# The second half of each modulation dot product on GpSimd and ScalarE instead of VectorE

## The chip, the cores and the metric

The program runs on one core of one Trainium2 chip. Its engines are TensorE (PE; PEld is its weight load), VectorE (DVE), ScalarE (ACT), GpSimd (POOL) and SyncE (SP), which issues most of the transfers. The metric is the device time of one execution in microseconds (us), the median of a few executions.

## What is computed

One transformer layer on 512 tokens of width 2048 in fp32: a modulation vector from the conditioning row `c`, a mixer (attention heads and a linear recurrence), and a layer of 16384 experts of which each token uses 128. Only the first lines matter here:

```python
sc = jax.nn.silu(c)                      # (1, 2048)
mod = sc @ w_ada[l] + b_ada[l]           # w_ada: (2048, 6 * 2048)
sh1, sc1, ga1, sh2, sc2, ga2 = jnp.split(mod, 6, axis=-1)
h = _rmsnorm(x, g_mix[l]) * (1.0 + sc1[:, None, :]) + sh1[:, None, :]
mix = _hybrid_mixer(h, w_in[l], ...)     # proj = h @ w_in, attention, recurrence, w_out
x = x + ga1[:, None, :] * mix
h = _rmsnorm(x, g_ffn[l]) * (1.0 + sc2[:, None, :]) + sh2[:, None, :]
x = x + ga2[:, None, :] * _peer(h, ...)
```

## The kernel before

**The dot products.** `w_ada` lies transposed, so that one block of 128 rows holds 128 outputs of `mod`, one in each partition, with their 2048 weights in a row. `ada(s, k)` makes the 128 outputs of block k of part s, and there are 96 such calls. Each call, a *pair* below, loads two tiles `araw` of 128x1024 (512 KB), one for each half of the 2048 weights, and reduces each against `sil`, which holds silu(c) in every partition: one VectorE instruction (L145, SCALAR_TENSOR_TENSOR) multiplies and sums along the row into `acc`. L147 adds the two sums and the bias into `mod`, and for two of the parts L151 makes a scale `gs` of it.

**Two stages use it.** In the prologue 32 pairs run, those of sh1 and sc1, in a loop over 16 blocks k of the model width. There `araw` has NAR = 5 buffers. Each k also normalizes and scales one block of `x` (L209 on ScalarE), splits it into a high and a low part (`hh` by a ScalarE cast at L210, `hlo` by a VectorE subtraction at L211), streams one tile of `w_pro`, which is split in the same way (`shi` at L91, `slo` at L92), and does 24 matmuls (L214, L217). In the mixer stage the other 64 pairs run, a few at a time by `some_ada` between the projections. There `araw` has two buffers. Each projection (`proj`, L299) streams two tiles of `w_in` through 4 buffers `raw` and 3 buffers for `shi` and `slo`, with 24 matmuls of 128x512 a tile. The values of these 64 pairs are wanted only later, at the output projection and beyond.

**The order.** The tile framework's scheduler sets the order on each engine from its own model of the program. The loads of `araw` (L144) and of the streams (L96) all stand in SyncE's queue, which issues in order: an instruction there that waits for a buffer holds back all that stand behind it. ScalarE, VectorE and GpSimd also work in order. GpSimd does nothing in the first 850 us but set constants; later it copies `dh` and `dl` (L674, L675) and issues the gathers of the expert layer.

Of the kernel before, what the change touches and what calls it, by code (L numbers as in the profile page):

```python
# [14 lines left out]
AF = mybir.ActivationFunctionType  # L15
OP = mybir.AluOpType
# [40 lines left out]
def program(ctx: ExitStack, tc: tile.TileContext, a):  # L57
    nc = tc.nc
    V, A, PE, G = nc.vector, nc.scalar, nc.tensor, nc.gpsimd
# [12 lines left out]
    def col(n, i):  # L72
        return cols[:, COFF[n] + i:COFF[n] + i + 1]
# [31 lines left out]
    def rstd(pool, ss, n, scale):  # L105
        v = pool.tile([128, 16], F32, name="rs", tag="rs", bufs=4)[:, :n]
        A.activation(v, ss, AF.Sqrt, bias=eps, scale=scale)
        V.reciprocal(v, v)
        return v
# [4 lines left out]
    acc = const.tile([128, 6, 16, 2], F32, name="acc")  # L114
# [16 lines left out]
    sil = silp.tile([128, D], F32, name="sil")  # L131
    crow = []
    for half in range(2):
        r = raw.tile([128, 1024], F32, name="raw")[:1]
# [5 lines left out]
    def ada(s, k):  # L140
        for half in range(2):
            r = araw[0].tile([128, 1024], F32, name="araw", bufs=NAR if araw[0] is pro_pool[0] else None)
            n0 = (s * 16 + k) * 128
            nc.sync.dma_start(r, a["w_ada"][n0:n0 + 128, half * 1024:half * 1024 + 1024])  # L144
            V.scalar_tensor_tensor(out=r, in0=r, scalar=1.0, in1=sil[:, half * 1024:half * 1024 + 1024],  # L145
                                   op0=OP.mult, op1=OP.mult, accum_out=acc[:, s, k, half:half + 1])
        V.scalar_tensor_tensor(out=mod[:, s, k:k + 1], in0=acc[:, s, k, 0:1], scalar=acc[:, s, k, 1:2],  # L147
                               in1=b_ada[:, s, k:k + 1], op0=OP.add, op1=OP.add)
        if s in (1, 4):
            g = col("g_mix" if s == 1 else "g_ffn", k)  # L150
            V.scalar_tensor_tensor(out=gsc[s - 1][:, k:k + 1], in0=mod[:, s, k:k + 1], scalar=1.0, in1=g,  # L151
                                   op0=OP.add, op1=OP.mult)
# [3 lines left out]
    def some_ada(n):  # L156
        for _ in range(n):
            if late_ada:
                ada(*late_ada.pop(0))
# [18 lines left out]
    with tc.tile_pool(name="pro", bufs=1, reuse_waits="tile") as pro:  # L178
# [7 lines left out]
        for t in range(NT):  # L186
# [7 lines left out]
            r = rstd(pro, ss, 1, 1.0 / D)  # L194
# [11 lines left out]
        for k in range(KC):  # L206
            ada(1, k)
            ada(0, k)
            A.activation(xT[:, k], xT[:, k], AF.Identity, bias=mod[:, 0, k:k + 1], scale=gsc[0][:, k:k + 1])  # L209
            A.copy(hh[k], xT[:, k])  # L210
            V.tensor_tensor(out=hlo[k], in0=xT[:, k], in1=hh[k], op=OP.subtract)  # L211
            wh, wl = stream(a["w_pro"][k], PRO * 128)
            for i, (l, r) in enumerate(three(wfh, wfl, hh[k], hlo[k])):
                PE.matmul(pf[:8], l[:, k * 8:k * 8 + 8], r, start=(k == 0 and i == 0), stop=(k == KC - 1 and i == 2))  # L214
            for j in range(PRO):
                for i, (l, r) in enumerate(three(wh, wl, hh[k], hlo[k])):
                    PE.matmul(pacc[j], l[:, j * 128:j * 128 + 128], r, start=(k == 0 and i == 0),  # L217
                              stop=(k == KC - 1 and i == 2))
# [43 lines left out]
    for t in range(NT):  # L262
# [3 lines left out]
                           scalar=-1.0, in1=bf_row[:, None, :].to_broadcast([128, NT, 8]), op0=OP.mult, op1=OP.subtract)  # L266
# [290 lines left out]
    with tc.tile_pool(name="wk2", bufs=12, reuse_waits="tile") as wk2:  # L557
        for q in range(4):
            pr = bank()
            for k4 in range(4):  # L560
                k = q * 4 + k4
# [79 lines left out]
    for h in range(H):  # L641
# [6 lines left out]
        for half in range(2):  # L648
            p = pbank()
            for hv in range(2):  # L650
                wh, wl = stream(a["w_q"][h * 2 + half, hv])
                for k8 in range(8):
                    k = hv * 8 + k8
# [12 lines left out]
            s = tp.tile([128, S], F32, name=f"sc{half}", bufs=2)  # L666
# [72 lines left out]
    with tc.tile_pool(name="tp0", bufs=1, reuse_waits="tile") as tp0:  # L739
# [9 lines left out]
        for h in range(H):  # L749
# [7 lines left out]
                               in1=se[:, 1].rearrange("p h k -> p (h k)"), op0=OP.mult, op1=OP.add)  # L757
# [112 lines left out]
    with tc.tile_pool(name="dz", bufs=1, reuse_waits="tile") as dz:  # L870
        Fs = []
        sets = {}
        for hf, (t, h0) in enumerate(((1, 0), (1, 64), (2, 0), (2, 64), (0, 0), (0, 64))):
            ws = dz.tile([128, NB, TH], F32, name="ws")
            for t4 in range(TH // 4):
# [5 lines left out]
                                in1=oT[t][:, 0, t0:t0 + 4, None].to_broadcast([128, 4, 128]), op=OP.is_equal)  # L881
# [34 lines left out]
    for n in range(2):  # L916
        tot = sets[n][2]
        V.scalar_tensor_tensor(out=ov[:, n:n + 1], in0=tot[:, 1:2], scalar=float(-LISTS[n][2] * 128), in1=tot[:, 2:3],
                               op0=OP.add, op1=OP.max)
# [86 lines left out]
    def inv(t):  # L1006
        ss = fin.tile([128, 1], F32, name="fss", bufs=4)
        V.tensor_reduce(ss, ssf[:, t], axis=AX.X, op=OP.add)
        return rstd(fin, ss, 1, 1.0 / D)
# [36 lines left out]
    r = inv(1)  # L1046
# [62 lines left out]
```

## Time and profile before

| | before |
|---|---|
| median of 3 executions | 3228.88 us (3227.6 to 3237.68) |
| the profiled execution | 3227.94 us, span 3226.1 us |
| PE busy | 2978.0 us (92%) |
| DVE busy | 2507.4 us (78%) |
| ACT busy | 1225.5 us (38%) |
| POOL busy | 959.5 us (30%) |
| L145, the 192 half products | 233.6 us of DVE, 1222 ns each |

The span runs from the first to the last instruction. Busy time is the time in which an engine executes; a share over the whole span is a mean over stages that have different limits, so the stages are read one by one. The modulation belongs to the first 552 us.

### The profile page before, as it was taken

How to read it: one execution, taken by the hardware profiler on the slowest of the kernel's cores; microseconds unless marked ns; L12 is line 12 of the kernel's file. 1: busy time of each engine (PE TensorE's matmuls, PEld its weight loads, DVE VectorE, ACT ScalarE, POOL GpSimd, SP SyncE). 2: the span in 40 equal slices, each digit the busy share in tenths (PEclk: the TensorE clock that was granted, in tenths of full speed). 3: DMA queues.
4: the chain of work that ended last, by engine and by line, in shares of the span. 5: the costliest groups of instructions: out<-in, count | busy, mean ns of one | idle time of the engine just before them, and what ended most of it. 6: DMA issues, size and time to landing. Idle time of an engine off the chain costs nothing. (4 is left out here: it accounts for less than half of the span.)

```text
span 3226.1 us, 40084 instructions
## 1 busy us (share of the span) xinstructions
PE 2978.0 (92%) x14597; PEld 2594.7 (80%) x14597; DVE 2507.4 (78%) x4073; ACT 1225.5 (38%) x1646; POOL 959.5 (30%) x668
## 2 busy tenths in 40 slices
PE   7899999989999999989899789999969999997787
PEld 6677778778788999989898789999957788886565
DVE  6877768762478899989999778888889855556787
ACT  5322224652322334334333222332233444444565
POOL 0000000000020002312225544444488644444774
PEclk9999899999999999989999899999989999998899
DMA  9777776243232457999998899999999976765996
GB/s 339 285 235 233 238 234 213 90 137 111 96 109 92 136 166 273 338 304 332 306 311 305 290 391 405 404 402 401 384 387 420 398 242 235 233 239 182 341 351 221
DMA packets 313124, 871.74 MB, mean 270 GB/s; under 512 B 125490, under 2 KB 164786, under 8 KB 258388
## 3 DMA queue, kind: packets, MB, share of 16 engines
q0 software_dynamic: 73376, 479.39, 39.0%
q1 hardware_dynamic: 239104, 389.52, 36.1%
q8 instruction: 116, 1.90, 0.2%
q14 instruction: 92, 0.75, 0.1%
q10 hardware_dynamic: 436, 0.18, 0.0%
HBM read 807.74 MB, written 61.25 MB: 269 GB/s over the span
## 5 line engine op out<-in xcount | busy, mean ns | idle before, releaser
L685 PE MATMUL pj<-dh,slo 128*128 128x384 f32 x2048 | 697.0, 341 | 39.4 <-DVE slo L92 38.9
L685 PE MATMUL pj<-dh,shi 128*128 128x384 f32 x2048 | 694.8, 339 | 12.2 <-ACT shi L91 12.2
L685 PE MATMUL pj<-dl,shi 128*128 128x384 f32 x2048 | 693.2, 338 | 0.0
L92 DVE TENSOR_TENSOR slo<-raw,shi 128x1024 fp32r<-128x1024 f32 (+1 forms) x402 | 485.4, 1215 | 237.3 <-ACT shi L91 235.8
L91 ACT CAST shi<-raw 128x1024 fp32r<-128x1024 f32 (+1 forms) x402 | 417.6, 1048 | 661.4 <-PE pj L685 256.1
L92 DVE TENSOR_TENSOR slo<-gr,shi 128x1024 fp32r<-128x1024 f32 x336 | 401.8, 1221 | 95.4 <-ACT shi L91 89.4
L685 PEld LDWEIGHTS pj<-dh,slo 128*128 128x128 f32 x2048 | 390.5, 191 | 45.3 <-DVE slo L92 44.9
L91 ACT CAST shi<-gr 128x1024 fp32r<-128x1024 f32 x336 | 342.0, 1046 | 204.3 <-PE ps L946 146.1
L685 PEld LDWEIGHTS pj<-dh,shi 128*128 128x128 f32 x2048 | 390.9, 191 | 13.9 <-ACT shi L91 13.7
L685 PEld LDWEIGHTS pj<-dl,shi 128*128 128x128 f32 x2048 | 390.2, 191 | 0.1
L946 PE MATMUL ps<-shi,gh 128*128 128x512 f32 x866 | 321.9, 412 | 69.3 <-ACT gh L91 55.2
L761 POOL DMA_INDIRECT gr<-u_rows,ei x128 | 200.5, 1567 | 526.1 <-DVE gr L775 295.4
L946 PE MATMUL ps<-slo,gh 128*128 128x512 f32 x866 | 350.8, 406 | 2.3 <-DVE slo L92 2.3
L946 PE MATMUL ps<-shi,gl 128*128 128x512 f32 x866 | 327.5, 402 | 13.2 <-DVE gl L92 13.2
L145 DVE SCALAR_TENSOR_TENSOR araw<-araw,sil 128x1024 f32<-128x1024 f32 x192 | 233.6, 1222 | 105.1 <-DMA araw<-w_ada 101.9
L773 DVE SCALAR_TENSOR_TENSOR y<-gr,dots,y 128x2048 f32<-128x2048 f32 x128 | 300.9, 2351 | 4.8 <-DMA gr<-v_rows,ei 2.7
L775 DVE SCALAR_TENSOR_TENSOR gr<-gr,hrow 128x2048 f32<-128x2048 f32 x128 | 290.7, 2282 | 14.0 <-DMA gr<-u_rows,ei 13.8
L761 POOL DMA_INDIRECT gr<-v_rows,ei x128 | 214.0, 1672 | 224.4 <-DVE y L773 189.7
L761 POOL DMA_INDIRECT raw<-tab,ig x159 | 246.0, 1547 | 112.6 <-DVE gl L92 82.5
L674 POOL CAST dh<-hh 128x384 fp32r<-128x384 f32 x16 | 10.4, 650 | 856.9 <-DVE hh L570 856.9
L946 PEld LDWEIGHTS ps<-shi,gh 128*128 128x128 f32 x866 | 168.2, 196 | 120.6 <-ACT gh L91 62.4
L761 POOL DMA_INDIRECT gr<-v_rows,iv x159 | 200.9, 1263 | 166.9 <-DVE slo L92 131.6
(345 smaller groups left out, 4955.8 us busy)
## 6 DMA issues: line engine op xcount, KB each, us to landing
raw<-peer_u SPq DMA_DIRECT2D x256, 512.0 KB, 8.1
araw<-w_ada SPq DMA_DIRECT2D x192, 512.0 KB, 5.2
raw<-w_in SPq DMA_DIRECT2D x66, 512.0 KB, 4.9
tab<-ws SPq DMA_DIRECT2D x24, 1024.0 KB, 13.0
raw<-w_out SPq DMA_DIRECT2D x32, 512.0 KB, 3.6
raw<-w_q SPq DMA_DIRECT2D x32, 512.0 KB, 3.6
tab<-ge SPq DMA_DIRECT2D x128, 128.0 KB, 5.2
tab<-ge SPq DMA_DIRECT2D x128, 64.0 KB, 6.4
```

The costliest lines, as they stand in the source:

```text
L91: A.copy(hi, src)
L92: V.tensor_tensor(out=lo, in0=src, in1=hi, op=OP.subtract)
L145: V.scalar_tensor_tensor(out=r, in0=r, scalar=1.0, in1=sil[:, half * 1024:half * 1024 + 1024], op0=OP.mult, op1=OP.mult, accum_out=acc[:, ...
L674: G.tensor_copy(dh[k], wh2[k][:, 128:])
L685: PE.matmul(p[:, :NDT], l[:, k8 * 128:k8 * 128 + 128], r, start=(k == 0 and i == 0), stop=(k == KC - 1 and i == 2))
L761: G.indirect_dma_start(out=out, out_offset=None, in_=src, in_offset=bass.IndirectOffsetOnAxis(ap=idx, axis=0))
L773: V.scalar_tensor_tensor(out=y0, in0=r, scalar=dots[:, j:j + 1], in1=y0, op0=OP.mult, op1=OP.add)
L775: V.scalar_tensor_tensor(out=r, in0=r, scalar=1.0, in1=hrow, op0=OP.mult, op1=OP.mult, accum_out=dots[:, j:j + 1])
L946: PE.matmul(banks[t][half * 2 + q2], l[:, ts], x[:, sl], start=first and i == 0, stop=last and i == 2)
```

## The change

The first half of each pair stays as it was. In the second half a GpSimd TENSOR_TENSOR multiplies the tile by `sil` in place, and a ScalarE activation (Identity, in place) copies it onto itself and sums it into `acc`.

```diff
-            V.scalar_tensor_tensor(out=r, in0=r, scalar=1.0, in1=sil[:, half * 1024:half * 1024 + 1024],
-                                   op0=OP.mult, op1=OP.mult, accum_out=acc[:, s, k, half:half + 1])
+            if half:
+                G.tensor_tensor(out=r, in0=r, in1=sil[:, 1024:], op=OP.mult)
+                A.activation(r, r, AF.Identity, accum_out=acc[:, s, k, 1:2])
+            else:
+                V.scalar_tensor_tensor(out=r, in0=r, scalar=1.0, in1=sil[:, :1024], op0=OP.mult, op1=OP.mult,
+                                       accum_out=acc[:, s, k, 0:1])
```

In the changed file the GpSimd product is L146, the ScalarE sum L147, the VectorE product L149, and every later line has a number that is 4 higher (L147 becomes L151, L299 becomes L303).

SyncE's queue in the mixer stage, near the 16th pair there, before. Of the two `araw` of a pair, whose numbers are 2 or 3 apart, the lower is the first half; in brackets stands what the load waits for, where DVE or Activation is the engine that used the buffer last and DMAHW a transfer far ahead in the queue:

```order
L96 DMA raw_2134<-w_in 128x1024 [waits DMAHW1_49,DVE_49]
L144 DMA araw_2660<-w_ada 128x1024 [waits DMAHW2_49,DVE_49]
L144 DMA araw_2663<-w_ada 128x1024 [waits DMAHW3_49,DVE_49]
L144 DMA araw_2837<-w_ada 128x1024 [waits DMAHW4_49,DVE_49]
L96 DMA raw_2164<-w_in 128x1024 [waits DMAHW5_49,DVE_49]
L144 DMA araw_2840<-w_ada 128x1024 [waits DMAHW6_49,DVE_49]
```

All of these buffers were given back by VectorE. The same place of the changed kernel:

```order
L96 DMA raw_2204<-w_in 128x1024 [waits DMAHW1_49,DVE_49]
L144 DMA araw_2635<-w_ada 128x1024 [waits DMAHW2_49,DVE_49]
L144 DMA araw_2705<-w_ada 128x1024 [waits DMAHW3_49,Activation_49]
L144 DMA araw_2708<-w_ada 128x1024 [waits DMAHW4_49,DVE_49]
L144 DMA araw_2883<-w_ada 128x1024 [waits DMAHW5_49,Activation_49]
L96 DMA raw_2244<-w_in 128x1024 [waits DMAHW6_49,DVE_49]
L144 DMA araw_2886<-w_ada 128x1024 [waits DMAHW7_49,DVE_49]
```

The first half of a pair (2705, 2883) now waits for ScalarE, and its second half (2708, 2886) for VectorE. Over the whole stage the order of loads is nearly the old one; behind the last `araw` 13 loads of `w_in` stood before, and 4 stand now.

ScalarE in the mixer stage, before, from an exponential of the softmax (L355) on:

```order
L91 CAST shi<-raw 128x1024
L355 ACTIVATE w,st<-ps,st 128x128
L330 COPY w<-pj 128x512
L91 CAST shi<-raw 128x1024 x2
L91 CAST wr<-pj 128x512
```

The changed kernel at such a place:

```order
L359 ACTIVATE w,st<-ps,st 128x256
L147 ACTIVATE araw,acc<-araw 128x1024
L91 CAST shi<-raw 128x1024
L359 ACTIVATE w,st<-ps,st 128x128
L334 COPY w<-pj 128x512
L147 ACTIVATE araw,acc<-araw 128x1024
L91 CAST shi<-raw 128x1024
L147 ACTIVATE araw,acc<-araw 128x1024
L91 CAST shi<-raw 128x1024
L91 CAST wr<-pj 128x512
```

The sums (L147) now stand between the casts of the stream and behind exponentials and copies of TensorE's results (`ps`, `pj`).

## Rows read from the trace of the kernel before

**Rows 1.** Windows by stage: PE, PEld, DVE, ACT, POOL busy us, clock, transfers.

```profile
core 0: us, PE busy (x) PEld busy (x) DVE busy (x) ACT busy (x) POOL busy (x), PEclk, DMA share, GB/s
46.00:142.00 96.00, 84.53 (x361) 62.04 (x360) 89.24 (x174) 32.31 (x42) 0.00 (x0) 1.00 0.92 338
152.00:550.00 398.00, 376.87 (x1625) 297.94 (x1624) 294.58 (x619) 118.30 (x211) 0.00 (x0) 0.93 0.71 234
550.00:655.00 105.00, 99.42 (x421) 78.29 (x419) 86.88 (x128) 71.44 (x103) 0.00 (x0) 0.98 0.28 89
655.00:3226.10 2571.10, 2379.28 (x12026) 2127.56 (x12025) 2012.06 (x3097) 965.63 (x1240) 958.81 (x662) 0.96 0.77 280
```

**Rows 2.** L145 over the span: ns min/median/max of one, first and last start.

```profile
L145 DVE SCALAR_TENSOR_TENSOR araw<-araw,sil x192: 1206/1224/1228, 18.7 to 550.4; 128x1024 f32<-128x1024 f32 x192
```

**Rows 3.** Waits of engines, 152 to 550 us: us in total, times, longest.

```profile
DVE araw L145 <- DMA araw<-w_ada: 99.4, 91, 2.9
ACT w L355 <- DVE st L353: 77.5, 19, 8.8
ACT mg L387 <- PE ps L384: 72.0, 8, 12.5
```

**Rows 4.** Timeline of DVE, 300 to 330 us: start, duration, operation, idle before.

```profile
311.40 1.23 DVE L145 SCALAR_TENSOR_TENSOR araw<-araw,sil 128x1024 f32<-128x1024 f32 x1 [0.19 <-DMA araw<-w_ada]
...
314.81 1.23 DVE L145 SCALAR_TENSOR_TENSOR araw<-araw,sil 128x1024 f32<-128x1024 f32 x1 [1.73 <-DMA araw<-w_ada]
...
317.72 1.23 DVE L145 SCALAR_TENSOR_TENSOR araw<-araw,sil 128x1024 f32<-128x1024 f32 x1
```

**Rows 5.** Timeline of SyncE's queue in the same stretch.

```profile
312.66 3.74 SPq L144 DMA_DIRECT2D araw<-w_ada  x2
...
318.98 3.90 SPq L144 DMA_DIRECT2D araw<-w_ada  x2
```

**Rows 6.** The loads of `araw` from 150 to 560 us.

```profile
L144 SPq DMA_DIRECT2D araw<-w_ada x128: 327/328/383, 152.6 to 546.0; - x128
...
DMA to landing us min/median/max: 3.7/4.8/5.9
```

**Rows 7.** L299 over the span: the first and the last matmul of `w_in`.

```profile
L299 PE MATMUL pj<-hh,slo x528: 387/396/628, 151.2 to 654.8; 128*128 128x512 f32 x176
```

**Rows 8.** Timeline of DVE in the prologue: one period of the loop over k.

```profile
101.11 1.09 DVE L92 TENSOR_TENSOR slo<-raw,shi 128x896 fp32r<-128x896 f32 x1 [0.34 <-ACT shi L91]
102.12 0.68 DVE L211 TENSOR_TENSOR hlo<-xT,hh 128x512 fp32r<-128x512 f32 x1
102.72 0.21 DVE L147 SCALAR_TENSOR_TENSOR mod<-acc,cols 128x1 f32<-128x1 f32 x1
...
108.18 1.09 DVE L92 TENSOR_TENSOR slo<-raw,shi 128x896 fp32r<-128x896 f32 x1 [0.35 <-ACT shi L91]
```

**Rows 9.** Timeline of POOL and DVE near 896 us.

```profile
895.42 0.52 POOL L675 CAST dl<-hlo 128x384 fp32r<-128x384 f32 x1
...
895.88 0.52 POOL L674 CAST dh<-hh 128x384 fp32r<-128x384 f32 x1
895.90 1.57 DVE L92 TENSOR_TENSOR slo<-raw,shi 128x1024 fp32r<-128x1024 f32 x1 [5.30 <-ACT shi L91]
896.33 1.51 POOL L675 CAST dl<-hlo 128x384 fp32r<-128x384 f32 x1
```

**Rows 10.** ScalarE: casts of the stream from 150 to 560 us.

```profile
L91 ACT CAST shi<-raw x52: 1036/1050/1067, 149.8 to 556.9; 128x1024 fp32r<-128x1024 f32 x52
```

**Rows 11.** ScalarE: the read of a row sum behind an activation, at L193.

```profile
L193 ACT ACTIVATION_READ_ACCUMULATOR junk<-xt x4: 186/190/194, 9.0 to 38.5; 128x1 f32 x4
```

**Rows 12.** Timeline of SyncE's queue: two loads issued back to back, from the first

```profile
28.53 0.81 SPq L190 DMA_DIRECT2D xt<-x  x2
```

**Rows 13.** Timeline of PE: two matmuls 128x512 in a row.

```profile
103.98 0.40 PE L217 MATMUL ps<-hlo,shi 128*128 128x512 f32 x1
...
104.21 0.40 PE L217 MATMUL ps<-hh,slo 128*128 128x512 f32 x1
```

## The prediction

> **What bounds the kernel now.** I read the windows by stage first, since the modulation runs only in the first 552 us: the prologue loop, the mixer stage with the other 64 pairs (152 to 550 us), the rest of the mixer to 655 us, and everything behind it [rows 1]. In the long last stretch VectorE is 78% busy, but the change takes nothing from it there. In the mixer stage PE is busy 376.87 of 398 us, VectorE 294.58 and GpSimd not at all. So VectorE is not full where the change relieves it, and at most 21 us of idle PE could be won.
>
> Then I read the waits and the timelines of that stage, to see what VectorE's 103 idle us are. They are waits for transfers: 91 waits of L145, 99.4 us together [rows 3]. The timeline shows why. A product ends at 311.40 + 1.23 = 312.63 us, SyncE issues the next load into that buffer at 312.66, and the product on this load starts at 317.72, a round of 6.32 us, while the other buffer does the same half a round later [rows 4, 5]. With two buffers this round is the pace of the pairs: 64 pairs from 152.6 us [rows 6] to 550.4 + 1.2 = 551.6 us [rows 2] are 6.23 us each. The load takes 4.8 us of it (median, 3.7 to 5.9) [rows 6]; the product takes 1.22. The loads of `w_in`, which feed PE, stand in the same queue between the loads of `araw`, so whatever lengthens this round starves PE as soon as the round is longer than PE's own need. That is the number to look for.
>
> In the prologue VectorE is busy 89.24 of 96 us, and the transfers 0.92 of it [rows 1]. One k takes 108.18 - 101.11 = 7.07 us there, back to back on VectorE [rows 8].
>
> **The round after the change.** Removed are 96 products of 1.22 us from VectorE; of these, 64 lie in the mixer stage, and they free about 64 x 1.3 = 83 us of an engine that waits there anyway. Nothing follows from that by itself. Added are 96 GpSimd products and 96 ScalarE sums, in series, each on a buffer that SyncE is waiting for.
>
> The order of loads (the part on the change) says which buffer waits for which. The first half of a pair is loaded into the buffer of the pair before's second half, so it waits for ScalarE's sum. The second half stands behind it in the queue, mostly with one `w_in` between. It takes the other buffer, long free, but it can't be issued earlier. So the rounds no longer overlap: the second half is loaded, multiplied on GpSimd, summed on ScalarE, and only then does the next pair's load go out. The round is a chain:
>
> - Issue of first half, `w_in`, second half: two steps of 0.81 - 0.33 = 0.48 us [rows 12, 6]: 1.0 us.
> - Load of the second half: 4.8 us [rows 6]. The three transfers now start together and could slow each other (up to 5.9), but the traffic per us falls, so I keep the median.
> - Wait for VectorE: at GpSimd's copies near 896 us, one copy starts 0.46 us after the other and lasts 0.52, but the copy that meets VectorE's `slo<-raw,shi` lasts 1.51 and ends, at 897.84, 0.37 us behind it; and that VectorE instruction takes 1.57 where it takes 1.22 elsewhere [rows 9]. So two such instructions exclude each other. The first half's product (1.22 us) starts about 1 us before the second half lands; 0.3 us are left of it.
> - The GpSimd product, an operation the trace doesn't have. The copy takes 0.46 us for 384 columns of one input, so 1024 columns take 1.2 us with one input. That is the lower bound. Two inputs at that price each are 2.4 us, the upper bound. The product reads two tensors, so I take 2.4.
> - The ScalarE sum: 1.05 us like a cast of that size [rows 10], and 0.19 us to read the sum [rows 11]: 1.2 us. Handing over from engine to engine, 0.1 us.
>
> Together 9.8 us in place of 6.23. On ScalarE 64 x 1.2 = 79 us join 118 busy of 398 [rows 1], so its load costs nothing; its order may (below).
>
> 64 x 9.8 = 627 us. PE cannot cover that: it does a `w_in` tile in 24 x 0.23 = 5.5 us [rows 13], and 66 tiles with all that lies between took 151.2 to 654.8 us [rows 7], 7.6 us each, which is 504 us in all. Loads of `w_in` come nearly once a pair, so PE will wait at each.
>
> **Prologue.** With five buffers the round is not the limit, but the exclusion is. For one k VectorE keeps two products of 1.22 [rows 2], `slo` for 1.01 and `hlo` for 0.60 [rows 8], 4.0 us, which now alternate with two GpSimd products of 2.4: 8.8 us in place of 7.07. Over the 13 periods of 96 us that is +22 us. With the cheap product it is 6.4 us, and the transfers, busy 0.92, would stop the gain at 6.5, which is 13 x 0.57 = -7 us. PE's 5.5 us for a k and ScalarE's two more sums are covered by this period.
>
> **Sum.** The stage starts at 152.6 + 22, its pairs take 627, and behind them the last tiles remain. Before, these took 654.8 - 551.6 = 103 us; 9 of the 13 loads of `w_in` that stood there now go earlier, 9 x 5.5 = 50 us, so 53 stay. 152.6 + 22 + 627 + 53 = 855, against 655: +200 us. What follows (2571 us) doesn't change but for a few swapped gathers, which I put at nothing. The profiled execution took 3227.9 us (its median 3228.9): **3428 us**.
>
> A rule that speaks against this change stands beside the exclusion: the Trainium skill, SBUF — State Buffer, section "Who interferes with whom", says that a VectorE instruction with two inputs in SBUF contends with a GpSimd instruction that reads SBUF, and that the second one is blocked entirely. The rows near 896 us bear this out for copies; without it the wait (64 x 0.3 = 19 us) and the prologue's 22 us would go, and the time would be 3387 us.
>
> For the product's price the Trainium skill, GPSIMD Engine Reference, section 3.1, gives 4497 ns for an addition of 2048 columns; half of it, an estimate, is 2.25 us, and the sum by it would be some 14 us lower. No row here shows it.
>
> **The rivals.**
>
> *The sums queue on ScalarE.* L147 stands behind exponentials that wait for a VectorE maximum (77.5 us) and copies that wait for PE (72.0) in this stage [rows 3]. Before, nothing that SyncE needs hung on them; now each such wait can sit in the round. All of it would give 3428 + 150 = 3578, half of it 3503. For it: the order puts sums there. Against: with PE starved, its results come early compared with the loads.
>
> *A cheap product without exclusion.* 1.2 us and no wait: a round of 8.3, 152.6 + 531 + 53 = 737, +82: 3310. For it: the lower bound of the copy's price. Against: the second input, and 896 us.
>
> *It is hidden.* The mixer would end where it did if the round were (655 - 152.6 - 53)/64 = 7.0 us or less. With the fastest load (3.7), the product at 1.2 and no waits it is 7.2, and 667 us, +12, less 7 in the prologue: 3233, no measurable change. It needs every bound at once.
>
> *VectorE's relief wins.* In the prologue, VectorE's own work falls by 2.4 us a k. If the transfers could follow, PE's 5.5 us would be the period: 13 x 1.57 = -20, 3208. It decides only if GpSimd's product doesn't exclude VectorE and the mixer's round stays below 7.0. The rows speak against both.
>
> **How the numbers follow.** The main case has 0.57 (3385 to 3475 by itself: a round between 9.2 and 10.5 us), the queue on ScalarE 0.21, the cheap product 0.13, hidden 0.06, the relief 0.03. From 3300 to 3540 us the hidden and relieved cases fall out below (0.09) with a little of the cheap one, and the upper part of the ScalarE queue above (0.07). About 0.3%, 10 us, is what a measurement can tell from no change. Slower by more: 0.57 + 0.21 + 0.13 = 0.91; within: 0.06; faster: 0.03.
>
> **What would show it.** Right: in the mixer stage SyncE's L144 waits for ScalarE, the first halves go out 9 to 10.5 us apart, PE has gaps before each `w_in` tile, and the last `araw` is used near 800 us; GpSimd's products last 2.2 to 2.6 us, longer where VectorE runs. The prologue's period is near 8.8 us. Wrong: if rounds of two pairs still overlap (loads 6 to 7 us apart), if the GpSimd product takes nearer 1.2 us, or if loads land in 4 us when less is in flight, the time is nearer 3300. If sums wait behind exponentials, it is over 3500.

## The result and the profile after

The changed kernel takes 3327.78 us (median of 4 runs, 3318.35 to 3334.31) against 3228.93 for the kernel before in the same comparison: a ratio of 1.0298, 95% interval 1.0267 to 1.0329. It is slower by 99 us, where the prediction said 200. The profiled execution is the slowest of the four, 3334.31 us, of which 3332.5 is the span.

Where the time went is read from the first and last matmul of each stage. The prologue is all that lies ahead of the first matmul of `w_in` (L299 before, L303 after), the mixer stage goes from there to the last one, then come `w_out` and `w_q`, the u-stage (matmuls of `peer_u`), and all that follows:

| us | prologue | mixer stage | `w_out` to `w_q` | u-stage | rest | span |
|---|---|---|---|---|---|---|
| before | 150.7 | 504.1 | 420.1 | 1267.3 | 883.9 | 3226.1 |
| after | 185.6 | 561.6 | 420.1 | 1273.9 | 891.3 | 3332.5 |
| difference | +34.9 | +57.5 | 0 | +6.6 | +7.4 | +106.4 |

So 92 of the 106 us lie in the two stages that hold the edited lines. The windows of after, for the stretches of [rows 1]:

```profile
core 0: us, PE busy (x) PEld busy (x) DVE busy (x) ACT busy (x) POOL busy (x), PEclk, DMA share, GB/s
46.00:142.00 96.00, 75.97 (x285) 54.63 (x283) 84.41 (x91) 47.66 (x76) 56.21 (x21) 0.86 0.77 261
152.00:550.00 398.00, 354.44 (x1458) 272.92 (x1456) 240.99 (x426) 158.59 (x286) 122.75 (x51) 0.89 0.56 193
550.00:655.00 105.00, 91.10 (x373) 72.06 (x372) 80.06 (x119) 52.04 (x88) 35.48 (x13) 0.91 0.59 200
```

VectorE is relieved in the mixer stage (240.99 against 294.58 of 398 us), and PE does less: 1458 matmuls in the records against 1625, at a granted clock of 0.89 against 0.93. Nothing is won by the relief, as the prediction had it.

The groups of the edited lines in the mixer stage of after, 186 to 692 us: busy time, mean ns of one, then the idle time ahead of them and what ended it.

```profile
L146 POOL TENSOR_TENSOR araw<-araw,sil 128x1024 f32<-128x1024 f32 x64 | 157.3, 2458 | 362.8 <-DMA araw<-w_ada 314.9 <-ACT shi L91 16.4 <-DVE wr L92 15.6
L149 DVE SCALAR_TENSOR_TENSOR araw<-araw,sil 128x1024 f32<-128x1024 f32 x64 | 129.5, 2023 | 151.2 <-DMA araw<-w_ada 151.2
L147 ACT ACTIVATE araw<-araw 128x1024 f32<-128x1024 f32 x64 | 67.9, 1061 | 243.3 <-POOL araw L146 243.3
L151 DVE SCALAR_TENSOR_TENSOR mod<-acc,cols 128x1 f32<-128x1 f32 x63 | 13.2, 210 | 5.8 <-ACT araw L147 4.5
```

GpSimd's product takes 2.46 us and ScalarE's sum 1.06: both as forecast. VectorE's product, which was 1.22 us [rows 2] and whose code is the same, now takes 2.02: the two engines hold each other up. ScalarE's sum waits for GpSimd's product alone (243.3 us) and hardly for anything else.

The timeline of after, one round and the start of the next: the lines on `araw`, of all engines and of SyncE's queue (start, duration, operation, idle time before):

```profile
380.21 0.81 SPq L144 DMA_DIRECT2D araw<-w_ada  x2
...
384.23 2.37 POOL L146 TENSOR_TENSOR araw<-araw,sil 128x1024 f32<-128x1024 f32 x1 [5.14 <-DMA araw<-w_ada]
385.47 2.21 DVE L149 SCALAR_TENSOR_TENSOR araw<-araw,sil 128x1024 f32<-128x1024 f32 x1 [1.43 <-DMA araw<-w_ada]
386.64 1.06 ACT L147 ACTIVATE araw<-araw 128x1024 f32<-128x1024 f32 x1 [4.15 <-POOL araw L146]
...
387.72 0.80 SPq L144 DMA_DIRECT2D araw<-w_ada  x2
...
391.95 2.36 POOL L146 TENSOR_TENSOR araw<-araw,sil 128x1024 f32<-128x1024 f32 x1 [5.35 <-DMA araw<-w_ada]
```

Two loads go out together at 380.21 us. The first is the second half of one pair: it lands 4.0 us later, GpSimd has it to 386.60, ScalarE to 387.70, and at 387.72 its buffer is loaded again. The other is the first half of the *next* pair, as the order of loads shows, where each second half is followed at once by the next first half (2708, 2883): VectorE's product on it starts at 385.47, is blocked by GpSimd's and ends at 387.68. So both buffers come free at the same time, after 7.5 us, and the rounds of neighbouring pairs do overlap. Over the stage the sums end at 691.5 us for the last pair, and the first load was issued at 187.6 us:

```profile
L147 ACT ACTIVATE araw<-araw x96: 1041/1060/1078, 25.1 to 691.5; 128x1024 f32<-128x1024 f32 x96
```

That is (692.6 - 187.6)/64 = 7.89 us for a pair, against 6.23 before and 9.8 forecast. The last matmul of `w_in` starts at 747.2 us, about 55 us later (forecast 53).

In the prologue VectorE is where it shows. The groups on VectorE in before, from 46 to 146 us:

```profile
L92 DVE TENSOR_TENSOR slo<-raw,shi 128x896 fp32r<-128x896 f32 (+1 forms) x15 | 16.6, 1109 | 8.2 <-ACT shi L91 8.1
L211 DVE TENSOR_TENSOR hlo<-xT,hh 128x512 fp32r<-128x512 f32 x15 | 10.3, 684 | 0.0
L147 DVE SCALAR_TENSOR_TENSOR mod<-acc,cols 128x1 f32<-128x1 f32 x27 | 5.8, 215 | 0.3
```

The same groups in e1_prologue_only (after's path in the prologue alone), from 46 to 180 us:

```profile
L151 DVE SCALAR_TENSOR_TENSOR mod<-acc,cols 128x1 f32<-128x1 f32 x28 | 28.5, 1020 | 5.2 <-ACT araw L147 5.2
L92 DVE TENSOR_TENSOR slo<-raw,shi 128x896 fp32r<-128x896 f32 (+1 forms) x15 | 24.4, 1625 | 5.7 <-ACT shi L91 5.5
L215 DVE TENSOR_TENSOR hlo<-xT,hh 128x512 fp32r<-128x512 f32 x16 | 21.6, 1351 | 5.8 <-ACT hh L214 5.7
```

All three VectorE instructions are drawn out beside GpSimd's products, the smallest most in proportion: the `mod` line, one column wide, takes 1020 ns in the mean instead of 215.

### The profile page after: what moved, and what is told of

It is laid out like the page before. It is cut to its first block, busy times and chain, and to the rows that moved or that the text cites. A ratio compares the mean times of both kernels' runs of the same rounds, so it can differ in the third digit from the quotient of the medians.

```text
span 3332.5 us, 40296 instructions
## 1 busy us (share of the span) xinstructions
PE 3017.7 (91%) x14597; PEld 2619.5 (79%) x14597; DVE 2521.9 (76%) x3881; ACT 1328.0 (40%) x1840; POOL 1196.3 (36%) x764
## 5 line engine op out<-in xcount | busy, mean ns | idle before, releaser
L92 DVE TENSOR_TENSOR slo<-raw,shi 128x1024 fp32r<-128x1024 f32 (+1 forms) x402 | 499.7, 1251 | 248.0 <-ACT shi L91 243.1
L146 POOL TENSOR_TENSOR araw<-araw,sil 128x1024 f32<-128x1024 f32 x96 | 243.3, 2535 | 446.9 <-DMA araw<-w_ada 370.1
L765 POOL DMA_INDIRECT gr<-u_rows,ei x128 | 207.4, 1620 | 525.7 <-DVE gr L779 296.5
L149 DVE SCALAR_TENSOR_TENSOR araw<-araw,sil 128x1024 f32<-128x1024 f32 x96 | 182.6, 1902 | 154.0 <-DMA araw<-w_ada 154.0
L765 POOL DMA_INDIRECT raw<-tab,ig x159 | 236.1, 1485 | 115.1 <-DVE gl L92 77.9
```

The costliest lines, as they stand in the source:

```text
L92: V.tensor_tensor(out=lo, in0=src, in1=hi, op=OP.subtract)
L146: G.tensor_tensor(out=r, in0=r, in1=sil[:, 1024:], op=OP.mult)
L765: G.indirect_dma_start(out=out, out_offset=None, in_=src, in_offset=bass.IndirectOffsetOnAxis(ap=idx, axis=0))
```

## The experiments

Twelve kernels were run, each beside the kernel before. Their stages, as differences to before in us from one profiled execution each:

| kernel | ratio to before, 95% interval | prologue | mixer | u-stage | rest |
|---|---|---|---|---|---|
| after | 1.0298 (1.0267-1.0329) | +34.9 | +57.5 | +6.6 | +7.4 |
| e1_prologue_only | 1.0305 (1.0270-1.0339) | +34.1 | -0.4 | +65.9 | -6.6 |
| e2_mixer_only | 1.0167 (1.0139-1.0195) | +0.1 | +58.3 | +3.8 | +3.6 |
| e3_three_buffers | 1.0364 (1.0339-1.0389) | +30.9 | +15.4 | +65.7 | +7.2 |
| e4_no_read | 1.0050 (1.0031-1.0069) | +6.1 | +27.0 | -1.9 | -9.6 |
| e5_writes_by_scalare | 1.0106 (1.0076-1.0136) | +38.1 | +0.5 | -8.5 | +3.8 |
| e6_control_writes | 1.0196 (1.0169-1.0224) | -0.5 | +3.7 | +63.0 | +12.3 |
| e7_shift_only | 0.9978 (0.9959-0.9997) | +8.6 | +2.2 | +4.2 | -9.4 |
| e8_vectore_product | 1.0204 (1.0173-1.0235) | +6.2 | -1.9 | +64.7 | +4.4 |
| e9_half_columns | 1.0073 (1.0049-1.0097) | +13.3 | +7.9 | +12.9 | +8.0 |
| e10_buffers_order | 1.0139 (1.0115-1.0163) | +32.9 | +12.4 | +2.3 | +6.1 |
| e11_before_three | 0.9982 (0.9968-0.9996) | -0.3 | +3.2 | +4.1 | +6.1 |
| e12_vectore_order | 0.9965 (0.9944-0.9987) | +5.3 | -8.8 | +3.4 | +1.5 |

`w_out` to `w_q` stays within 3.2 us in all. The last column moves between -9.6 and +12.3 us, and by 3.6 in e2, whose order of instructions from the u-stage on is that of before word for word; it is not explained here. Where the code of a stage is that of before, the prologue moves by up to 0.5 us and the mixer stage by up to 3.7 (e6). The kernel before took 3228.93, 3234.53, 3237.17 and 3243.09 us in its four comparisons and was profiled in the first alone, so the differences of a row need not add up to its ratio (e9: 41 us, against 0.73%, which is 24).

### e1 and e2: the two stages apart

```diff
-            if half:
+            if half and s < 2:     # e1_prologue_only
+            if half and s > 1:     # e2_mixer_only
```

VectorE's branch takes either half then, as before.

> GpSimd product and ScalarE sum only for the 32 pairs of the prologue; the 64 pairs of the mixer stage as before. Theory (two separate costs, one a stage): the first w_in matmul comes at 185.6 us as in the changed kernel, against 150.7 before, so +35 us and nothing else: 3264 us (3255 to 3272). Rival (the late start is caught up, since PE has slack behind the prologue): 3230 us.

> GpSimd product and ScalarE sum only for the 64 pairs of the mixer stage; the prologue as before. Theory (the two araw buffers are held longer, a round of 7.6 to 7.9 us a pair): the stage from first to last w_in matmul is 562 us against 504, +58: 3287 us (3275 to 3300). Rival (the mixer stage suffers only because the prologue leaves it nothing loaded ahead): under 3250.

Measured: 3290.22 us for e2, as expected, and 3328.25 for e1, 64 us above what was expected. The prologue and the mixer stage add up to after's (34.1 + 58.3 = 92.4, against 92.4), but e1 lost 65.9 us more in the u-stage, which holds nothing of the edit. That was a new question, taken up with e5 below.

### e3: a third buffer

```diff
-    araw[0] = pool(mix, "araw", 2)
+    araw[0] = pool(mix, "araw", 3)
```

and `WK = 17`, to make room for it.

> The changed kernel with three araw buffers in the mixer stage in place of two, and WK = 17 in place of 18 to make room. Theory (the round of the two buffers is the limit there): the +58 us of that stage fall to 10 or less, the prologue's +35 stay: 3265 to 3275 us. Rival (VectorE and GpSimd excluding each other is the limit, whatever the buffers): 3315 us or more.

The mixer stage lost 15.4 us instead of 57.5, its pairs took (539.0 - 176.4)/64 = 5.7 us, and the time was worse nonetheless, by 65.7 us in the u-stage. GpSimd's product stayed as long (2.61 us in the mean), but what it holds up on VectorE changed, as the groups of e3 from 190 to 535 us show:

```profile
L149 DVE SCALAR_TENSOR_TENSOR araw<-araw,sil 128x1024 f32<-128x1024 f32 x63 | 81.0, 1286 | 55.0 <-DMA araw<-w_ada 54.6
L151 DVE SCALAR_TENSOR_TENSOR mod<-acc,cols 128x1 f32<-128x1 f32 x62 | 65.9, 1063 | 0.5
L92 DVE TENSOR_TENSOR slo<-raw,shi 128x1024 fp32r<-128x1024 f32 x41 | 64.0, 1560 | 4.4 <-ACT shi L91 4.4
```

The half product is nearly free of it (1286 ns instead of 2023), and the `mod` line (1063 instead of 210) and `slo` have it now. So the engines still exclude each other, and yet 42 of the 57 us are gone: these hung on the ring of two buffers. The held-up half product was a part of that ring, and its share of the 42 us isn't separated.

### e4: GpSimd as long, but reading nothing

```diff
-                G.tensor_tensor(out=r, in0=r, in1=sil[:, 1024:], op=OP.mult)
+                for n in (1024, 1024, 640):
+                    G.memset(r[:, :n], 0.5)
```

The second half's product is left out.

> GpSimd's product is left out; in its place three memsets (1024, 1024 and 640 columns, some 2.3 us) write the tile and read nothing, and ScalarE sums as in the changed kernel. Theory (exclusion costs the prologue, the length of the chain costs the mixer): VectorE's half products fall from a median of 2.04 to 1.22 us, the prologue's +35 fall to 10 or less, the mixer's round stays near 7.5 us (4.0 load + 2.4 + 1.06): 3228.9 + 10 + 50 = about 3289 us. Rival A (exclusion is the cost in both stages): 3240. Rival B (exclusion costs nothing in either): 3328.

The groups of e4, 0 to 700 us:

```profile
L147 POOL MEMSET araw<- 128x1024 f32 x192 | 183.8, 957 | 399.8 <-DMA araw<-w_ada 288.2 <-ACT wr L91 17.1 <-DVE wr L92 13.2
L150 DVE SCALAR_TENSOR_TENSOR araw<-araw,sil 128x1024 f32<-128x1024 f32 x96 | 117.5, 1224 | 170.1 <-DMA araw<-w_ada 160.5 <-POOL araw L147 9.4
...
L147 POOL MEMSET araw<- 128x640 f32 x96 | 60.8, 633 | 5.5
...
L152 DVE SCALAR_TENSOR_TENSOR mod<-acc,cols 128x1 f32<-128x1 f32 x96 | 20.8, 217 | 34.2 <-ACT araw L148 34.0
```

GpSimd holds a buffer for 2 x 0.957 + 0.633 = 2.55 us, a little longer than the product did, and VectorE's instructions are back at 1224 and 217 ns: nothing is blocked. The prologue loses 6.1 us instead of 34.9, so 29 of the 35 were exclusion. Of the mixer's 57.5 us 27.0 remain. The pace of the pairs hardly fell (the last sum starts at 650.8 us: 7.7 us a pair); the rest of the gain is that the stage ended 36 us behind the ring and not 55. Which share of that is exclusion isn't separated here. The time, 3250.26 us, lies well below the 3289 that were expected: more of the loss hangs on exclusion, and on what lies behind the ring, than I had taken.

### e8 and e9: a shorter product

```diff
-                G.tensor_tensor(out=r, in0=r, in1=sil[:, 1024:], op=OP.mult)
+                V.tensor_tensor(out=r, in0=r, in1=sil[:, 1024:], op=OP.mult)              # e8_vectore_product
+                G.tensor_tensor(out=r[:, :512], in0=r[:, :512], in1=sil[:, 1024:1536], op=OP.mult)   # e9_half_columns, WK = 16
```

> The change with the second half's product on VectorE instead of GpSimd (a plain tensor-tensor product, an estimate of 1.1 to 1.3 us from the 1.22 us of the combined instruction), the sum still on ScalarE. No GpSimd instruction of the change is left, so no exclusion; the chain stays in three steps. Theory (two costs: exclusion, and the longer chain of the second half): prologue +6 us (as e4_no_read), round of the mixer stage 4.4 + 1.2 + 1.06 + 0.2 = 6.9 us instead of 7.5, that is +25 to +45 us; and, by this kernel's order on SyncE (four loads, then four writes, as in e1_prologue_only and e3_three_buffers), +66 us in the u-stage: 3229 + 6 + 35 + 66 = 3336 us (3320 to 3350). Rival A, GpSimd is not what costs, only the chain: mixer +58 us, 3359 us. Rival B, the order on SyncE has no part in it: 3270 us.

> The change with GpSimd's product over 512 of the half's 1024 columns only (the other 512 are summed without having been multiplied: that part of the product is left out), and 16 instead of 18 wk buffers, with which ScalarE's order in the u-stage keeps a cast of the next block ahead of each GELU, as in the kernel before. Theory: both losses have a threshold. In the mixer stage the ring of pairs may take up to 7.0 us a pair before it is later than the rest of the stage (it ends about 55 us ahead of the stage's end after the change; 64 x 7.03 + 55 = 504 us); the round of 7.87 us falls by the 1.2 us of product saved to 6.7 us, so the stage stays at 504 us within 8. In the prologue VectorE's busy time and GpSimd's product add up for a step: 6.57 - 2 x 1.22 + 2 x 1.2 = 6.5 us, below the 7.07 us of before, so +6 us as in e4_no_read and e8_vectore_product. u-stage 1260 to 1277 us. Time 3229 + 6 + 0 to 8 = 3239 us (3228 to 3250). Rival: the loss goes with GpSimd's time: half of 35 and of 58 us, 3276 us.

The product on VectorE took 1.22 us, and the last sum of e8 started at 605.7 us:

```profile
L146 DVE TENSOR_TENSOR araw<-araw,sil 128x1024 f32<-128x1024 f32 x64 | 78.3, 1224 | 62.9 <-DMA araw<-w_ada 62.5
...
L147 ACT ACTIVATE araw<-araw x96: 1045/1060/1077, 24.4 to 605.7; 128x1024 f32<-128x1024 f32 x96
```

That is (606.8 - 158.9)/64 = 7.0 us a pair, slower than before's 6.23, and the mixer stage lost nothing (-1.9 us; 25 to 45 were expected). So there is a threshold near where the prediction put it: e8's ring of 7.0 us a pair is hidden, e4's of 7.7 costs 27 us and after's of 7.9 costs 57. The longer chain alone, with product and sum on two engines, is free in the mixer stage. The u-stage lost 64.7 us, as expected, but by luck: the forecast put it down to SyncE's order, which is not the cause (see e5 below). The ratio is 3295 us on the base of 3229, not 3336.

In e9 the pace was 7.0 us a pair as well, the mixer stage lost 7.9 us and the prologue 13.3, against 6 forecast for the prologue. The ratio, 1.0073, is 3253 us on the base of 3229: just above the range of the threshold theory (3228 to 3250), far below the 3276 of proportional loss. The pace was not the 6.7 us forecast but at the threshold, which may be why the mixer stage was not quite free; the 7 us too many in the prologue and the 12.9 us of the u-stage (1280.1 us, 1260 to 1277 forecast) are not explained.

### e7: half of the prologue's products

```diff
-            if half:
+            if half and s == 0:
```

> After's path only for the shift pairs of the prologue (s = 0, 16 of the 96 pairs), everything else as before; in this kernel SyncE's order of loads and writes in the u-stage is as before (one write pair after three loads, one after one). Theory: about half of the 34 us of the prologue, that is +17 us (10 to 25), mixer and u-stage unchanged, 3246 us (3238 to 3256). Rival: what is lost in the prologue comes back with interest in the u-stage (66 us for 34 us in e1_prologue_only): 3246 + 33 = 3279 us or more.

Sixteen of the 32 products cost 8.6 us, not 17, and the u-stage lost nothing to speak of (+4.2). So the first of the two products of a step cost 8.6 us, and the second the other 26 of after's 35. The time, 3229.58 us beside 3237.17 for before, is below the range and 0.2% below before, which is less than what a measurement tells from no change.

### e5, e6, e10, e12: the 66 us of the u-stage

e1 and e3 lost 66 us where nothing was edited. The two kernels share an order of instructions there that before and after don't have. The first theory was SyncE's: in e1 four loads of `peer_u` stand together and then the writes of two blocks' results, which hold the next loads up.

```diff
-        nc.sync.dma_start(tab2[rows, 0:256], ge[:, 128:384])
-        nc.sync.dma_start(tab1[rows, 0:128], ge[:, 0:128])
+        nc.scalar.dma_start(tab2[rows, 0:256], ge[:, 128:384])
+        nc.scalar.dma_start(tab1[rows, 0:128], ge[:, 0:128])
```

> The kernel of e1_prologue_only with one edit more: the two writes of each u block's result are issued on ScalarE's DMA queue instead of SyncE's. Theory: the 66 us that e1_prologue_only lost in the u-stage (1332.9 us against 1267.0) are no cost of GpSimd's products, which are long over by then. They come from SyncE's order: there four loads of peer_u stand together and then four writes, for two blocks; the second block's writes wait for its end, and no load is issued for some 10 us in every pair of blocks (2129.69 to 2139.88), so a pair of blocks takes 18.8 us instead of 16.65. With the writes off that queue the loads never wait behind them: u-stage 1260 to 1277 us, prologue still +34, time 3229 + 34 = 3263 us (3250 to 3275). Rival: the loss is carried from the prologue or comes from GpSimd's gathers in their new order: u-stage stays near 1333 us and the time near 3328 us.

> The kernel before with only the writes of each u block's result issued on ScalarE's DMA queue: the control for e5_writes_by_scalare. In the kernel before TensorE is busy for all of that part of the u-stage, so the theory expects 3229 us within 10 (3219 to 3239), u-stage 1257 to 1277 us. Rival: the writes cost time in SyncE's order of before as well: u-stage shorter by 20 us or more, 3209 us or less.

e5 came out as the theory said: 3264.69 us (3263 forecast), the u-stage 74 us shorter than in e1. But the control contradicts the theory: the same edit made the kernel before 63 us slower in the u-stage, with nothing but loads of `peer_u` left in that part of SyncE's queue. So the writes on SyncE were not the cause, and e5 met its forecast by luck. What e1, e3, e6 and e8 have in common is on ScalarE. TensorE stops there, in e1 near 2137 us (ScalarE's lines, then PE's):

```profile
2128.80 0.49 ACT L693 ACTIVATE ge<-pj 128x384 f32<-128x384 f32 x1 [3.28 <-PE pj L689]
...
2137.17 0.49 ACT L693 ACTIVATE ge<-pj 128x384 f32<-128x384 f32 x1 [7.88 <-PE pj L689]
2137.56 2.93 ACT L91 CAST shi<-raw 128x1024 fp32r<-128x1024 f32 x3
...
2138.65 0.45 PE L689 MATMUL pj<-dh,shi 128*128 128x384 f32 x1 [1.56 <-ACT shi L91]
```

The GELU of a block (L693) waits 7.88 us for the block's last matmul, and the first cast of the next block stands behind it in ScalarE's order. So PE has nothing to do from the end of one block until GELU and cast are done. The windows of e1 around the stop, and last the longer one from 2100 to 2300 us:

```profile
2126.00:2130.00 4.00, 4.00 (x25) 4.00 (x25) 3.96 (x4) 0.49 (x1) 1.37 (x1) 1.00 1.04 402
2137.00:2140.70 3.70, 1.50 (x7) 1.09 (x7) 2.07 (x2) 3.32 (x4) 0.00 (x0) 1.00 0.96 394
2140.80:2144.00 3.20, 3.20 (x12) 3.20 (x11) 3.20 (x3) 0.00 (x0) 0.48 (x1) 0.50 1.00 382
...
2100.00:2300.00 200.00, 187.36 (x1009) 183.83 (x1010) 147.04 (x86) 52.60 (x65) 77.98 (x41) 0.95 0.94 351
```

The same long window of before:

```profile
2100.00:2300.00 200.00, 200.00 (x1156) 200.00 (x1155) 168.86 (x97) 58.40 (x72) 85.33 (x49) 1.00 1.02 402
```

Before, PE has no gap in 200 us. In e1 it is busy 1.50 of 3.7 us, and right behind that the granted clock is 0.50 (1.2 instead of 2.4 GHz) for the 3.2 us shown, though PE is busy throughout. Such a stop costs 2.2 us of idle time and another 1.6 at half speed, 3.8 us.

Counted in the order of ScalarE's instructions, over the first 127 of the 128 blocks: GELUs that have no cast of the next block ahead of them, in all and among blocks 80 to 126, beside the loss in the u-stage.

```
kernel                 in all   80 to 126   u-stage, us
before                    3         0           0
after                     3         0          +6.6
e2_mixer_only             3         0          +3.8
e4_no_read                0         0          -1.9
e5_writes_by_scalare      0         0          -8.5
e7_shift_only             0         0          +4.2
e1_prologue_only         18        13         +65.9
e3_three_buffers         18        12         +65.7
e6_control_writes        11         9         +63.0
e8_vectore_product       19        14         +64.7
```

The four that lose are the four with such GELUs in the late blocks. In e1 each of the 13 late ones has a stop of 2.2 us of PE behind it, and PE has no idle time behind the other blocks from 80 to 126. With 15 such GELUs more than before, e1 owes them 15 x 3.8 = 57 of its 65.9 us. The windows of the whole u-stage give the full sum (before, e1, e6):

```profile
1074.90:2342.50 1267.60, 1195.11 (x6942) 1181.41 (x6940) 1131.09 (x1586) 421.94 (x496) 410.34 (x255) 0.97 0.90 327
1108.30:2441.80 1333.50, 1226.43 (x6942) 1205.34 (x6940) 1122.76 (x1583) 421.55 (x496) 421.81 (x252) 0.95 0.88 309
1077.70:2408.30 1330.60, 1218.76 (x6942) 1199.56 (x6940) 1117.57 (x1577) 428.25 (x496) 407.98 (x251) 0.95 0.87 308
```

For the same 6942 matmuls PE is idle 107.1 us in e1 where it was idle 72.5, and busy 31.3 us longer, at a mean granted clock of 0.95 instead of 0.97: 34.6 + 31.3 = 65.9 us. Two more kernels were then chosen by this count alone, with other buffer counts and none there (e10: 2 in all; e12: 3):

```diff
-WK = 17
+WK = 16          # e10_buffers_order: e3_three_buffers with this
```

```diff
-WK = 18
+WK = 17          # e12_vectore_order: e8_vectore_product with this
-    araw[0] = pool(mix, "araw", 2)
+    araw[0] = pool(mix, "araw", 3)
```

> e3_three_buffers (the change with three araw buffers instead of two in the mixer stage) with 16 instead of 17 wk buffers: in ScalarE's order of the u-stage every GELU then has at least one cast of the next block ahead of it, where in e3_three_buffers one GELU in four had none. Theory: e3's u-stage of 1332.6 us came from that order alone: u-stage 1260 to 1277 us, prologue +31 to +35, mixer stage 515 to 525 us, so 3229 + 33 + 15 + 3 = 3280 us (3266 to 3292). Rival: the third buffer or GpSimd's products cost the 66 us: 3345 us again.

> e8_vectore_product (second half's product on VectorE, sum on ScalarE) with three araw buffers in the mixer stage and 17 wk buffers; in ScalarE's order of the u-stage every GELU now has at least one cast of the next block ahead of it (in e8_vectore_product one in four had none). Theory: prologue +6 us, mixer stage 502 us within 8, u-stage 1260 to 1277 us instead of e8's 1332: 3235 us (3225 to 3247). Rival: the sum on ScalarE, not the order, costs the 65 us in the u-stage: 3300 us.

Both lost nothing more in the u-stage (+2.3 and +3.4 us). e10 came out where expected, at a ratio of 1.0139, which is 3274 us on the base of 3229; e12 took 3228.60 beside 3243.09 for before in the same comparison, which is 3218 on that base and 7 us below its range. Its mixer stage was 7 us shorter than forecast, but the stages of its profile add up to +0.7 us against before's, so where it beats before is not shown. So the 66 us are ScalarE's order, which the scheduler happened to choose, and neither GpSimd nor the prologue; after escaped them. In e6, 11 such GELUs cost nearly as much as 18 in e1, because the stops are longer. The two writes that were moved to ScalarE stand between GELU and cast there (ScalarE's lines of one stop, then PE's):

```profile
2115.68 0.49 ACT L689 ACTIVATE ge<-pj 128x384 f32<-128x384 f32 x1 [5.66 <-PE pj L685]
2116.20 0.33 ACTq L691 DMA_DIRECT2D tab<-ge  x1
2116.56 0.45 ACTq L692 DMA_DIRECT2D tab<-ge  x1
2117.11 2.95 ACT L91 CAST shi<-raw 128x1024 fp32r<-128x1024 f32 x3 [0.94 <-ACT ge L689]
...
2118.21 0.44 PE L685 MATMUL pj<-dh,shi 128*128 128x384 f32 x1 [2.56 <-ACT shi L91]
```

PE waits 2.56 us for that cast where it waited 1.56 in e1. By the windows above, e6's 63 us are 39.3 us more of idle PE and 23.7 us more of busy PE.

With three buffers in the mixer stage, e10 lost 12.4 us there, where GpSimd has the product, and e12 won 8.8, where VectorE has it. So some 21 us are GpSimd's own even without the ring of two, by its length and its exclusion together.

### e11: the third buffer without the change

```diff
-    araw[0] = pool(mix, "araw", 2)
+    araw[0] = pool(mix, "araw", 3)
```

and `WK = 17`, on the kernel before.

> The kernel before with three araw buffers in the mixer stage (and 17 instead of 18 wk buffers): the control for the third buffer and a version that might be faster than both. Theory: in the kernel before the ring ends at 550 us, about 50 us before it would hold up the stage's end at 655, so a shorter round gives nothing: mixer stage 504 us within 8, 3229 us within 10. Rival: TensorE's 21 us of idle time from 152 to 550 us come from waits for the pairs on SyncE's queue: the stage shortens to about 485 us, 3210 us.

The mixer stage took 3.2 us longer, not shorter, and the time is 0.2% below before, which is no difference that this measurement can tell. The ring was not the limit before. The lowest ratio of all is e12's: 0.35% faster than before (interval 0.13 to 0.56%), with 495 us in the mixer stage, and little above the 0.3% that a measurement can tell.

## Why the prediction was right and wrong

The measured 3327.78 us lies within the stated 3300 to 3540 us, but near the lower end, which was left for the cheap product, and that did not come. The sum of the main case, 3428 us, missed by 100.

**The bound.** Right. VectorE waited for transfers, its relief gave nothing, and the pace of the pairs against PE's need decides: e3, e8 and e11 show it from three sides, and the 7.0 us at which the prediction put the threshold is where e8's ring still runs without loss.

**The round after the change.** This step failed. It was put at 9.8 us and measured 7.5 in the timeline and 7.89 over the stage. The failing sentence is that the second half "takes the other buffer, long free" and that "the rounds no longer overlap". The order shows for each load which engine frees its buffer, and I took for a first half's buffer that of the pair just before. It is the one before that: a second half follows its own pair's first half in one buffer (VectorE frees it), and the first half of the pair after next follows it (ScalarE frees it). So two chains run side by side, one per buffer, and the loads of a second half and of the next first half go out together. With that, the first of the terms, 1.0 us of issue, and the 0.3 of waiting are gone, and the load of a second half takes 4.0 us instead of 4.8. Whether it is quicker because less is in flight (193 GB/s against 234 [rows 1]) or because it goes out ahead of the other is not shown; the first half that goes out with it is taken up 1.2 us later, at 385.47. The sum for the timeline's round is 4.0 + 2.4 + 1.1 = 7.5; the 0.4 us up to the mean of the stage are not taken apart here. The shorter round takes 64 x (9.8 - 7.89) = 122 us off the 200 forecast; the prologue adds 13 and the later stages 14 that were not in it, and that gives the 106 us of the profile within 2 us. The prediction named overlapping rounds, loads of 4 us and a time nearer 3300 as what would prove it wrong, and that is what came.

**Product, sum and exclusion.** Right in size: 2.46 us for the product (2.4 taken, between bounds of 1.2 and 2.4), 1.06 + 0.19 for the sum. The row of two copies near 896 us [rows 9] carried over to a product of two inputs. The Trainium skill, SBUF — State Buffer, section "Who interferes with whom", has a VectorE instruction with two inputs in SBUF contend with a GpSimd instruction that reads SBUF, and not with one that only writes it. The trace agrees: VectorE's half took 2.02 us in the mean where it had taken 1.22, and 1.22 in e4, in which GpSimd only writes.

**Prologue.** Right in cause, too small: +35 against +22. The loop has 16 steps and I counted the 13 of the window: 16 x 1.73 = 28. From the first `slo` of `w_pro` to the sixteenth it took 100.7 us before (28.7 to 129.4) and 127.9 after (30.7 to 158.6), +27; a step grew from 6.7 us in the mean to 8.5. (Before, only the later steps took the 7.07 us that the prediction read off; some of the earlier ones took 5.6.) The other 8 us lie ahead of the loop and behind it, and no run here takes them apart. That e7 paid 8.6 us for the first product of a step, and after 35 for two, agrees with a sum on VectorE that has to pass the 7.07 us of before.

**The last tiles and the later stages.** The 53 us behind the last pair were right (55). The traces have 12 and 3 loads of `w_in` behind the last `araw` where 13 and 4 were counted; the difference of 9 is the same. The later stages were put at nothing; after lost 14 us there, in stretches that move by as much between kernels without a loss of their own.

**The rivals.** The sums did not queue on ScalarE: in the mixer stage all but two of the 64 started within 0.04 us of the end of GpSimd's product. The cheap product without exclusion fell on both counts. The hidden case came true in e8's mixer stage, with a product of 1.22 us on VectorE.

## What to carry to other kernels

When a step is given to a slower engine, find the pace at which it would be seen, and draw the occupants of each buffer in turn for three rounds before calling steps serial: which load waits for which use two rounds back decides whether chains overlap. In e8 a reduction in two instructions over the same buffer cost the mixer stage nothing while its ring stayed at that pace; GpSimd's share of it, in after, also stretched what VectorE did meanwhile. And compare stages, not totals: a scheduler may reorder a far stage for any small edit, and here an accident of order cost more than either part of the change.

## What the hardware showed that was not expected

A stop of TensorE is paid twice. After a stretch of 3.7 us in which it was busy for 1.50, the granted clock was 0.50 for 3.2 us, and matmuls stood 0.32 us apart instead of 0.17, although PE was busy again; at 1.6 of 3.8 us a stop, that is two fifths of what the stops in e1 cost.

Exclusion is worst, in proportion, for the shortest instruction. One of VectorE's that is one column wide and takes 0.21 us took 1.02 in the mean beside GpSimd's products, and GpSimd's product itself was held up to 4.70 us in after. GpSimd's memset of 1024 columns took 0.96 us and blocked nothing.
